# Softmax division moved behind P times V in both attentions of a two-layer hybrid decoder

## The chip, the cores and the metric

One Trainium2 chip, and one of its cores. The time is device time of one launch, in microseconds. The core has five engines that run beside each other, each in the order of its own queue: TensorE (PE; its weight loads are shown apart as PEld), VectorE (DVE), ScalarE (ACT), GpSimd (POOL) and SyncE (SP), which here issues nearly all DMAs. Engines wait for each other through semaphores. TensorE writes to PSUM, of which there are eight banks of 2 KB per partition; everything else lives in SBUF.

## What is computed

A trunk of two equal layers on one sequence of 1024 tokens, width 1024, all float32. Each layer normalises its input, projects it once to 1312 columns, and feeds three mixers from that: a sliding-window attention (window 128, six query heads, two key heads, a learned sink per head), a pooling mixer, and a causal latent attention (MLA, six heads). Their outputs are joined by one output projection, and a SwiGLU feed-forward block follows. The two softmaxes are what the change is about:

```python
# sliding window: per block of 128 queries, keys of this block and of the one before
s = jnp.where(mask, s + bias, -jnp.inf)
lse = jnp.logaddexp(jax.nn.logsumexp(s, axis=-1, keepdims=True), sk)   # sk: the sinks
p = jnp.exp(s - lse)
o = jnp.einsum('bnhgqk,bnkhd->bnqhgd', p.astype(v.dtype), vb)
# MLA: per block of 128 queries, all keys up to it
s = jnp.where(k_idx[None, :] <= qi[:, None], s, -jnp.inf)
p = jax.nn.softmax(s, axis=-1)
return jnp.einsum('bhqk,bkhd->bqhd', p.astype(v.dtype), v)
```

In both, a row of exponentials is divided by its sum (in the first, the sum holds the sink's term too) and then multiplied by V.

## The kernel before

Matrix products are split in two or three: an operand is rounded to a shorter float32 type (`hi`), the remainder is kept as `lo`, and hi·hi, hi·lo and lo·hi (or two of them) are summed in PSUM. The helper `split` (line 58) does this with one ScalarE cast and one VectorE subtraction, so all splits carry line 58.

Each layer has three phases. **`phase1`** (line 283) runs over eight tiles `t` of 128 tokens: normalise, transpose, project (lines 381 to 383), pooling mixer, and at its end the sliding-window attention of this tile. **`phase2`** (line 545) makes queries, keys and values of the MLA in `gen(t)`, and runs its attention in four sweeps `s` of 256 queries (two blocks `j` of 128); between heads it works off the output projection (`early_out`, at line 816 and lines 795 to 797, and `late_out`, line 819). **`phase34`** is the feed-forward block; it takes about 640 of the 1105 us of a layer and the change does not touch it.

**Sliding-window attention of one tile** (lines 503 to 541), for each of two groups `g` of three heads: QK to PSUM (513, 514); VectorE adds the bias into `Pt` (516) and takes the row maximum (518); ScalarE takes the exponentials, three instructions, whose row sums land in `sm` (521); VectorE takes the reciprocals (523); ScalarE multiplies `Pt` by them, three instructions (526); TensorE transposes `Pt` in 128-key blocks into the PSUM tile `tp` (532; pool `ps_tp`, one buffer); `split` makes `pT` from it; PV goes to `po` (536, 537), which holds the output transposed: value channels on partitions, queries along the free axis. The upper 64 partitions of `po` hold the product with V's remainder; ScalarE copies them to `ob` (539) and VectorE adds both halves into `xm[:, t, 0:3]` (540).

**MLA attention** (`attn`, lines 705 to 773), one head at a time: QK per block `j` (729 to 733); maximum (735, or 738 for the last sweep); exponentials with row sums (742; where the keys take two PSUM banks there are two sums, added at 744); reciprocal (746); `Pt` times the reciprocal (748), on VectorE for `j == 0` and in the third sweep for every third head's `j == 1`, else on GpSimd; transposes (756; `ps_tp`, two buffers), `split`, PV (765, 766), and the same joining of two halves (768, 770) into 64 partitions of `xm[:, 2s:2s+2, 5 + h//2]`. Two heads share a column of `xm`, one in each half of the partitions.

**What sets the order.** The program is written as one stream, and a planner in the framework (line 1295, `schedule_with_timeline_sim=True`) orders each engine's queue: it plays the program through with its own costs, and of the instructions that are ready takes the one earliest in the program, apart from those that the code pins (`issue_after`) or gives another place in that order (`high_priority`, as for `early_out`). So other instructions, or other durations in the planner's eyes, can give another order. SBUF is handed out as a stack of pools; `phase1` and `phase2` start at the same address, and a tile of a later phase waits for the tiles that lay at its place. Two dummy pools (`gap`, lines 298 and 302) move what stands above them.

**How the attention ends.** The first feed-forward weights are loaded to the place where `phase2` holds its small tiles (pool `late`: maxima, sums, `ob`), so this load (line 1102) waits for the last head. `late_out` reads `xm` of the last two tiles after it.

Of the kernel before, what the change touches and what calls it, by code (L numbers as in the profile page):

```python
# [11 lines left out]
F32 = mybir.dt.float32  # L12
# [3 lines left out]
AF = mybir.ActivationFunctionType  # L16
ALU = mybir.AluOpType
# [4 lines left out]
P = 128  # L22
# [260 lines left out]
def phase1(nc, tc, A, l, pool, split, f, bcast, G, setup):  # L283
    ve, sc, gp, te, sy = nc.vector, nc.scalar, nc.gpsimd, nc.tensor, nc.sync
    cosT, sinT = G["cosT"], G["sinT"]
    ident, xm, xrow, krr = G["ident"], G["xm"], G["xrow"], G["krr"]
    with ExitStack() as ph:
        gap = G["gap"]
        two = pool(ph, f"p1b_{l}", bufs=2)
        one = pool(ph, f"p1_{l}")  # L290
# [20 lines left out]
        ps_tp = pool(ph, f"p1tp_{l}", bufs=1, space=PSUM)  # L311
# [30 lines left out]
        with tc.high_priority() if l == 0 else nullcontext():  # L342
            if l == 0:
                head(0)
            for i, (c0, n) in enumerate(((0, 512), (512, 400), (912, 400))):
                for k in range(KT):
# [3 lines left out]
                    g = gn[:, k : k + 1]  # L350
# [10 lines left out]
        for g in range(4):  # L361
            o = 64 * (g % 2)
# [8 lines left out]
        for t in range(NT):  # L371
# [133 lines left out]
            for g in range(2):  # L505
                gs = slice(3 * g, 3 * g + 3)
                Pt = two.tile([P, 3, 264], F32, name="Pt")
                gp.tensor_copy(Pt[:, :, nk : nk + 1], G["sinks"][:, l, gs].unsqueeze(2))
                for i0, ni in ((0, 2), (2, 1)):
                    s = ps_sc.tile([P, 2, 256], F32, name="s")  # L510
                    for i in range(i0, i0 + ni):
                        h = 3 * g + i
                        te.matmul(s[:, i - i0, 0:nk], qs[:, h], kr5[:, 0, g, k0 : k0 + nk], start=True, stop=False)
                        te.matmul(s[:, i - i0, 0:nk], qs[:, h], kr5[:, 1, g, k0 : k0 + nk], start=False, stop=True)
                    h0 = 3 * g + i0
                    ve.tensor_tensor(out=Pt[:, i0 : i0 + ni, 0:nk], in0=s[:, 0:ni, 0:nk],
                                     in1=G["bias"][:, h0 : h0 + ni, 256 - nk : 256], op=ALU.add)
                ve.tensor_reduce(mx[:, gs], Pt[:, :, 0 : nk + 1], AX.X, ALU.max, negate=True)
                for i in range(3):
                    h = 3 * g + i  # L520
                    sc.activation(Pt[:, i, 0 : nk + 1], Pt[:, i, 0 : nk + 1], AF.Exp, bias=mx[:, h : h + 1],
                                  accum_out=sm[:, h : h + 1])
                ve.reciprocal(sm[:, gs], sm[:, gs])
                for i in range(3):
                    h = 3 * g + i
                    sc.activation(Pt[:, i, 0:nk], Pt[:, i, 0:nk], AF.Copy, scale=sm[:, h : h + 1])
                po = ps_o.tile([P, 512], F32, name="po")
                nb = nk // P
                for b in range(nb):
                    tp = ps_tp.tile([P, 4, P], F32, name="tp")  # L530
                    for i in range(3):
                        te.transpose(tp[:, i], Pt[:, i, b * P : (b + 1) * P], ident)
                    pT = two.tile([P, 2, 3, P], F32R, name="pT")
                    split(pT[:, 0], pT[:, 1], tp[:, 0:3])
                    vv = (vt if b == nb - 1 else vprev)[:, g].rearrange("p a d -> p (a d)")
                    te.matmul(po[:, 0:384], vv, pT[:, 0].rearrange("p a b -> p (a b)"), start=b == 0, stop=False)
                    te.matmul(po[:, 0:384], vv, pT[:, 1].rearrange("p a b -> p (a b)"), start=False, stop=b == nb - 1)
                ob = one.tile([P, 384], F32, name="ob")
                sc.copy(ob[0:64], po[64:128, 0:384])
                ve.tensor_tensor(out=xm[64 * g : 64 * g + 64, t, 0:3], in0=po[0:64, 0:384].rearrange("p (a b) -> p a b", a=3),  # L540
                                 in1=ob[0:64].rearrange("p (a b) -> p a b", a=3), op=ALU.add)
            vprev = vt


def phase2(nc, tc, A, l, pool, split, f, bcast, G):
# [3 lines left out]
    with ExitStack() as ph:  # L549
# [155 lines left out]
        def attn(s, heads):  # L705
            qTs = [q2[2 * s], q2[2 * s + 1]]
            for h in heads:
                Ps = []
                for j in range(2):
                    t = 2 * s + j  # L710
                    valid = (t + 1) * P
# [26 lines left out]
                        ve.tensor_reduce(mx[:, 0:1], outs[0][0], AX.X, ALU.max, negate=True)  # L738
                    if len(outs) == 2:
                        ve.tensor_tensor(out=mx[:, 0:1], in0=mx[:, 0:1], in1=mx[:, 1:2], op=ALU.min)  # L740
                    for i, (o, c0, n) in enumerate(outs):
                        sc.activation(Pt[:, c0 : c0 + n], o, AF.Exp, bias=mx[:, 0:1], accum_out=sm[:, i : i + 1])
                    if len(outs) == 2:
                        ve.tensor_tensor(out=sm[:, 0:1], in0=sm[:, 0:1], in1=sm[:, 1:2], op=ALU.add)
                    sm = sm[:, 0:1]
                    ve.reciprocal(sm, sm)
                    eng = ve if j == 0 or s == 2 and h % 3 == 0 else gp
                    eng.tensor_scalar(out=Pt[:, 0:valid], in0=Pt[:, 0:valid], scalar1=sm, scalar2=None, op0=ALU.mult)
                    Ps.append(Pt)
                po = ps_o.tile([P, 512], F32, name="po")  # L750
                for c in range(s + 1):
# [19 lines left out]
                    out=xm[r0 : r0 + 64, 2 * s : 2 * s + 2, 5 + h // 2],  # L771
                    in0=po[0:64, 0:256].rearrange("p (a b) -> p a b", a=2),
                    in1=ob[0:64].rearrange("p (a b) -> p a b", a=2), op=ALU.add)

        def both(s):
            streams = [gen(2 * s), gen(2 * s + 1)] if s < 4 else []
# [522 lines left out]
```

## Time and profile before

| | |
|---|---|
| time, median of 3 runs | 2216.93 us (2209.97 to 2217.36) |
| the profiled execution | 2210.4 us, span 2208.6 us, mean granted TensorE clock 0.985 |
| PE busy | 2114.1 us (96%), 10468 instructions |
| DVE busy | 1692.3 us (77%), 2595 |
| ACT busy | 1087.7 us (49%), 2300 |
| POOL busy | 976.2 us (44%), 916 |

All stages below are given in us from the span's start. The sliding-window attention runs in 45 to 241 and again in 1130 to 1350, the MLA sweeps in 241 to 445 and 1345 to 1545. A matmul's busy time includes its way through the array, and the next one starts long before it ends, so a PE that is 96% busy may still have room; the chain of waits, which follows the last instruction back to what released it, says better where PE sets the time. Windows give each engine's busy time in a stretch, with the number of instructions in brackets.

### The profile page before, as it was taken

To read this page: it belongs to the slowest core of one execution; us is meant where nothing else is said; L and a number is where in the kernel's file an instruction comes from. 1 tells how busy PE (TensorE), PEld (TensorE's weight loads), DVE (VectorE), ACT (ScalarE), POOL (GpSimd) and SP (SyncE) were. 2 spreads that over 40 slices of the span, in tenths; PEclk is the share of its full clock that TensorE was granted. 3 is DMA by queue.
4 is the path that set the end of the run, shared out by engine and by line. 5 is a ranking of instruction groups with operands and counts; after the bars stand their busy time and mean duration, and the time that the engine had idled before them with its cause. 6 is when DMAs were issued, how large, how long until landed. Compare 5 with 4: busy or idle time off the path is not lost.

```text
span 2208.6 us, 29772 instructions
## 1 busy us (share of the span) xinstructions
PE 2114.1 (96%) x10468; PEld 1766.5 (80%) x10468; DVE 1692.3 (77%) x2595; ACT 1087.7 (49%) x2300; POOL 976.2 (44%) x916
## 2 busy tenths in 40 slices
PE   7998999999999999999989988999999999999999
PEld 5887788877788888788868867988778888887887
DVE  5567888898988787765845678887998888877657
ACT  5778767563434333311257786665634343343111
POOL 1433647245544452532614344462465444425215
PEclk8999999999999999999999999999999999999999
DMA  7002221323534435975530022113234443359754
GB/s 220 1 1 80 82 77 39 106 96 133 181 134 166 149 125 198 412 296 188 200 113 1 1 95 77 68 49 102 96 144 165 144 171 134 142 217 412 278 200 162
DMA packets 137932, 312.16 MB, mean 141 GB/s; under 512 B 17297, under 2 KB 68152, under 8 KB 137784
## 3 DMA queue, kind: packets, MB, share of 16 engines
q1 hardware_dynamic: 137784, 310.27, 39.4%
q8 instruction: 83, 1.36, 0.3%
q14 instruction: 65, 0.53, 0.1%
HBM read 203.53 MB, written 106.70 MB: 140 GB/s over the span
## 4 chain that ended last, share of the span: by engine, by line
PE 70%; DVE 10%; DMA 8%; ACT 6%; POOL 3%; issue 2%; SPq 1%; ACTq 0%; POOLq 0%; DVEq 0%
PE gu L1149 10%; PE gu L1147 10%; PE gu L1148 10%; PE dn L994 5%; PE dn L996 5%; PE dn L995 5%; PE acc L381 3%; PE acc L382 3%; PE acc L383 3%; DMA rw<-in_w_down_dram 2%; PE tp L756 2%; DMA raw<-in_w_in_dram 1%; PE ss L732 1%; PE po L766 1%; DMA raw<-in_w_gate_dram 1%
## 5 line engine op out<-in xcount | busy, mean ns | idle before, releaser
L1149 PE MATMUL gu<-T,sb 128*128 128x512 f32 x704 | 274.8, 391 | 9.8 <-DVE sb L58 9.7
L1147 PE MATMUL gu<-T,sb 128*128 128x512 f32 x704 | 274.9, 390 | 4.6 <-ACT sb L58 2.5
L1148 PE MATMUL gu<-T,sb 128*128 128x512 f32 x704 | 274.0, 389 | 0.0
L994 PE MATMUL dn<-op,ga 128*128 128x512 f32 x616 | 241.3, 393 | 7.4 <-DMA ga<-gd 7.4
L995 PE MATMUL dn<-op,ga 128*128 128x512 f32 x616 | 241.4, 392 | 0.0
L996 PE MATMUL dn<-op,ga 128*128 128x512 f32 x616 | 240.6, 392 | 0.0
L58 ACT CAST go<-xm 128x512 fp32r<-128x512 f32 x154 | 95.1, 620 | 274.4 <-POOL xm L1181 94.2
L943 POOL TENSOR_TENSOR rw<-rw 128x1536 f32<-128x1536 f32 (+1 forms) x32 | 112.4, 3522 | 257.0 <-DVE op L953 163.5
L1124 POOL TENSOR_TENSOR xm<-raw 128x512 f32<-128x512 f32 x44 | 68.6, 1561 | 319.9 <-DMA raw<-in_w_up_dram 122.8
L952 ACT CAST op<-rw 128x1536 fp32r<-128x1536 f32 (+1 forms) x56 | 76.9, 1376 | 266.7 <-PE dn L996 253.8
L58 DVE TENSOR_TENSOR go<-xm,go 128x512 fp32r<-128x512 f32 x154 | 154.4, 1012 | 34.1 <-ACT go L58 30.1
L58 ACT CAST sb<-raw 128x512 fp32r<-128x512 f32 x180 | 110.4, 617 | 122.5 <-PE gu L1149 99.6
L1149 PEld LDWEIGHTS gu<-T,sb 128*128 128x128 f32 x704 | 132.1, 188 | 41.3 <-DVE sb L58 13.9
L1147 PEld LDWEIGHTS gu<-T,sb 128*128 128x128 f32 x704 | 132.2, 188 | 34.5 <-ACT sb L58 4.6
L1181 POOL TENSOR_TENSOR xm<-xm 128x512 f32<-128x512 f32 x88 | 143.3, 1637 | 30.4 <-DVE go L58 19.6
L1148 PEld LDWEIGHTS gu<-T,sb 128*128 128x128 f32 x704 | 132.2, 188 | 27.4
L58 DVE TENSOR_TENSOR sb<-raw,sb 128x512 fp32r<-128x512 f32 x180 | 152.9, 850 | 1.0
L953 DVE TENSOR_TENSOR op<-rw,op 128x1536 fp32r<-128x1536 f32 (+1 forms) x56 | 113.8, 2032 | 40.0 <-ACT op L952 40.0
L994 PEld LDWEIGHTS dn<-op,ga 128*128 128x128 f32 x616 | 116.7, 189 | 33.3 <-issue 7.3
L1147 PE MATMUL gu<-B,A 128*128 128x512 f32 x336 | 132.1, 393 | 4.4 <-ACT B L58 4.4
L995 PEld LDWEIGHTS dn<-op,ga 128*128 128x128 f32 x616 | 116.7, 189 | 24.4
L996 PEld LDWEIGHTS dn<-op,ga 128*128 128x128 f32 x616 | 116.7, 189 | 24.3
(322 smaller groups left out, 6102.5 us busy)
## 6 DMA issues: line engine op xcount, KB each, us to landing
gd<-go SPq DMA_DIRECT2D x154, 512.0 KB, 3.1
ga<-gd SPq DMA_DIRECT2D x154, 512.0 KB, 5.7
raw<-in_w_gate_dram SPq DMA_DIRECT2D x22, 1024.0 KB, 5.6
raw<-in_w_up_dram SPq DMA_DIRECT2D x22, 1024.0 KB, 6.5
rw<-in_w_down_dram SPq DMA_DIRECT2D x44, 512.0 KB, 8.1
xp<-xt SPq DMA_DIRECT2D x32, 256.0 KB, 2.0
old<-xp SPq DMA_DIRECT2D x16, 512.0 KB, 4.1
xp<-xm SPq DMA_DIRECT2D x16, 512.0 KB, 2.9
```

What stands on the lines that cost most here:

```text
L58: return sc.copy(hi, src), ve.tensor_tensor(out=lo, in0=src, in1=f(hi), op=ALU.subtract)
L943: gp.tensor_tensor(out=o, in0=a, in1=b, op=ALU.subtract)
L952: sc.copy(t[:, 0], q[b])
L953: ve.tensor_tensor(out=t[:, 1], in0=q[b], in1=f(t[:, 0]), op=ALU.subtract)
L994: te.matmul(acc, S_[:, j, 0, ts], T_[:, 0, j], start=j == 0, stop=False)
L995: te.matmul(acc, S_[:, j, 0, ts], T_[:, 1, j], start=False, stop=False)
L996: te.matmul(acc, S_[:, j, 1, ts], T_[:, 0, j], start=False, stop=j == h - 1)
L1124: gp.tensor_tensor(out=s1, in0=q["A21"], in1=q["A22"], op=ALU.add)
L1147: te.matmul(acc, s[:, 0, k], b[:, 0, k], start=k == 0, stop=False)
L1148: te.matmul(acc, s[:, 0, k], b[:, 1, k], start=False, stop=False)
L1149: te.matmul(acc, s[:, 1, k], b[:, 0, k], start=False, stop=k == HK - 1)
L1181: gp.tensor_tensor(out=q[o], in0=q[a], in1=q[b], op=op)
```

## The change

Neither attention scales `Pt` any more: the products with V run on the bare exponentials, and the finished output is multiplied by the reciprocal of the row sums. Since the output lies transposed (queries along the free axis), the reciprocals have to lie so too: they are spread over 64 columns per head by a GpSimd copy (`rec`), transposed by TensorE into a PSUM tile of the pool that the `Pt` transposes use, and VectorE multiplies `xm` in place by that tile. In phase 1 this is done once per tile, for all six heads: one reciprocal, one copy of 128x384, three transposes, one multiplication of 128x384. In phase 2 it is done once per pair of heads and sweep: one reciprocal of four sums, one copy of 128x256, two transposes, one multiplication of 128x256. The new tiles are `rec` (1536 bytes per partition, pool `one` of phase 1; 1024 bytes, pool `late` of phase 2) and `sums` (two buffers, pool `late`).

```diff
 # phase1, for each group g
-                ve.reciprocal(sm[:, gs], sm[:, gs])
-                for i in range(3):
-                    h = 3 * g + i
-                    sc.activation(Pt[:, i, 0:nk], Pt[:, i, 0:nk], AF.Copy, scale=sm[:, h : h + 1])
 ...
 # phase1, after both groups
+            ve.reciprocal(sm, sm)
+            rec = one.tile([P, 3, 2, 64], F32, name="rec")
+            gp.tensor_copy(rec, sm.rearrange("p (g i) -> p i g", g=2).unsqueeze(3).to_broadcast([P, 3, 2, 64]))
+            tp = ps_tp.tile([P, 4, P], F32, name="tp")
+            for i in range(3):
+                te.transpose(tp[:, i], rec[:, i].rearrange("p g d -> p (g d)"), ident)
+            ve.tensor_tensor(out=xm[:, t, 0:3], in0=xm[:, t, 0:3], in1=tp[:, 0:3], op=ALU.mult)
 ...
 # phase2, attn
+                if h % 2 == 0:
+                    G["sums"] = late.tile([P, 2, 2], F32, name="sums", bufs=2)
+                sums = G["sums"]
 ...
+                    total = sums[:, j, h % 2 : h % 2 + 1]
                     for i, (o, c0, n) in enumerate(outs):
-                        sc.activation(Pt[:, c0 : c0 + n], o, AF.Exp, bias=mx[:, 0:1], accum_out=sm[:, i : i + 1])
+                        sc.activation(Pt[:, c0 : c0 + n], o, AF.Exp, bias=mx[:, 0:1],
+                                      accum_out=sm[:, i : i + 1] if len(outs) == 2 else total)
                     if len(outs) == 2:
-                        ve.tensor_tensor(out=sm[:, 0:1], in0=sm[:, 0:1], in1=sm[:, 1:2], op=ALU.add)
-                    sm = sm[:, 0:1]
-                    ve.reciprocal(sm, sm)
-                    eng = ve if j == 0 or s == 2 and h % 3 == 0 else gp
-                    eng.tensor_scalar(out=Pt[:, 0:valid], in0=Pt[:, 0:valid], scalar1=sm, scalar2=None, op0=ALU.mult)
+                        ve.tensor_tensor(out=total, in0=sm[:, 0:1], in1=sm[:, 1:2], op=ALU.add)
 ...
+                if h % 2:
+                    ve.reciprocal(sums, sums)
+                    rec = late.tile([P, 2, 2, 64], F32, name="rec")
+                    gp.tensor_copy(rec, sums.unsqueeze(3).to_broadcast([P, 2, 2, 64]))
+                    tp = ps_tp.tile([P, 512], F32, name="tp")
+                    for j in range(2):
+                        te.transpose(tp[:, j * P : (j + 1) * P], rec[:, j].rearrange("p a d -> p (a d)"), ident)
+                    o = xm[:, 2 * s : 2 * s + 2, 5 + h // 2]
+                    ve.tensor_tensor(out=o, in0=o, in1=tp[:, 0 : 2 * P].rearrange("p (a b) -> p a b", a=2), op=ALU.mult)
```

## The prediction

> **What bounds the kernel now.** I read the page first, then the windows by stage, then the chain of waits stage by stage. The page:
>
> ```profile
> span 2208.6 us, 29772 instructions
> PE 2114.1 (96%) x10468; PEld 1766.5 (80%) x10468; DVE 1692.3 (77%) x2595; ACT 1087.7 (49%) x2300; POOL 976.2 (44%) x916
> PE 70%; DVE 10%; DMA 8%; ACT 6%; POOL 3%; issue 2%; SPq 1%; ACTq 0%; POOLq 0%; DVEq 0%
> ```
>
> TensorE sets 70% of the time, so whatever the change adds there counts where PE leads. Where it leads is seen in the windows of the attention stages (PE, PEld, DVE, ACT, POOL busy with counts; granted clock; DMA) and in the chain of three of them (70 to 185, 185 to 240, 325 to 375):
>
> ```profile
> 45.00:185.00 140.00, 135.77 (x783) 118.35 (x782) 86.50 (x201) 100.79 (x284) 53.15 (x120) 0.99 0.05 18
> 185.00:241.00 56.00, 48.00 (x259) 39.24 (x258) 46.89 (x94) 45.43 (x120) 29.24 (x54) 0.97 0.33 108
> 241.00:325.00 84.00, 81.77 (x498) 72.50 (x499) 71.55 (x169) 57.93 (x142) 44.01 (x44) 1.00 0.20 70
> 325.00:375.00 50.00, 45.48 (x307) 40.03 (x306) 45.54 (x115) 39.75 (x106) 33.19 (x32) 1.00 0.16 59
> 375.00:442.00 67.00, 66.66 (x432) 59.53 (x430) 54.37 (x87) 38.45 (x75) 23.36 (x19) 1.00 0.28 95
> 1279.00:1350.00 71.00, 60.39 (x306) 49.04 (x305) 53.75 (x108) 49.81 (x132) 29.86 (x50) 0.93 0.29 96
> 1431.00:1474.00 43.00, 38.92 (x245) 34.82 (x244) 36.63 (x92) 33.34 (x88) 33.18 (x32) 0.89 0.11 38
> ```
> ```profile
> by line: PE acc L382 23.7%; PE acc L383 23.6%; PE acc L381 23.6%; PE tq L406 4.6%; PE tp L532 4.5%; PE s L513 3.6%; PE th L339 3.2%; PE s L514 3.1%; PE po L536 2.8%; PE po L537 2.7%; PE ta L448 1.4%; PE ta L460 0.8%; DVE Pt L516 0.6%; PE po
> by line: DMA raw<-in_w_out_dram 12.8%; ACT Pt L526 9.0%; ACT Pt L521 8.1%; issue 6.9%; POOL ms L115 4.7%; ACT wo L58 4.3%; DVE ms L657 4.1%; ACT mh L58 3.4%; ACT qbh L577 3.1%; ACT pT L58 3.1%; ACT ob L539 2.7%; ACT kvh L577 2.4%; DVE ropea
> by line: DVE mx L735 12.4%; ACT Pt L742 11.7%; DVE pT L58 6.9%; issue 6.7%; ACT pT L58 5.9%; DMA raw<-in_w_out_dram 5.3%; PE ss L729 4.7%; PE ss L732 4.6%; PE ss L733 4.4%; DVE ms L657 3.4%; DVE Pt L748 3.3%; DVE kT L58 2.8%; POOL wot L834
> ```
>
> Each layer has two kinds of stretch. In three of them PE leads: the sliding window's first six tiles (45 to 185), the first two MLA sweeps (241 to 325) and the last (375 to 442). In two it doesn't: the **tail** of phase 1 (185 to 241, and 1279 to 1350), where ScalarE, DMA, and in layer 1 also POOL, take turns, and the **middle** of the MLA (325 to 375, and 1431 to 1474), where DVE is busy 91% and 85% of the time. The change takes work from ACT, DVE and POOL and gives some to PE: it can only earn in the loose stretches and must pay in the tight ones.
>
> **What is removed.** The first row is phase 1's scaling, the next two phase 2's, the last its reciprocal:
>
> ```profile
> L526 ACT ACTIVATE Pt<-Pt,sm x96: 389/497/528, 56.7 to 1325.3; 128x256 f32<-128x256 f32 x84, 128x128 f32<-128x128 f32 x12
> L748 DVE TENSOR_SCALAR Pt<-Pt,sm x52: 270/552/1155, 251.8 to 1518.8; 128x128 f32<-128x128 f32 x12, 128x384 f32<-128x384 f32 x12, 128x640 f32<-128x640 f32 x12, 128x896 f32<-128x896 f32 x12
> L748 POOL TENSOR_SCALAR Pt<-Pt,sm x44: 924/1604/3138, 253.1 to 1526.1; 128x256 f32<-128x256 f32 x12, 128x512 f32<-128x512 f32 x12, 128x1024 f32<-128x1024 f32 x12, 128x768 f32<-128x768 f32 x8
> L746 DVE RECIPROCAL sm<-sm x96: 134/156/167, 251.6 to 1525.9; 128x1 f32<-128x1 f32 x96
> ```
>
> That is 96 x 0.497 = 48 us off ACT, about 30 us off DVE beside 15 us of reciprocals, and some 75 us off POOL.
>
> **What is added.** Per tile of phase 1 (16 of them) one reciprocal, one POOL copy of 128x384, three transposes and one product of 128x384; per head pair and sweep (24) one reciprocal, one copy of 128x256, two transposes and one product of 128x256. The nearest rows are the four-transpose group of line 339 in the chain, a single transpose of line 756 by its own duration, POOL's broadcast copy, and the additions into `xm`, which also read PSUM with 384 and 256 elements per partition (they use 64 partitions; DVE's time goes by the free size in the rows that I compare, so I take them as they are):
>
> ```profile
> 84.39 0.44 PE th L339 x4
> L756 PE MATMUL tp<-ident,Pt x432: 270/273/449, 253.4 to 1540.6; 128*128 128x128 f32 x144
> L663 POOL COPY kn<-krr x16: 343/348/713, 209.9 to 1413.0; 128x192 f32<-128x192 f32 x16
> L540 DVE TENSOR_TENSOR xm<-po,ob x32: 540/550/553, 68.3 to 1346.9; 64x384 f32<-64x384 f32 x32
> L770 DVE TENSOR_TENSOR xm<-po,ob x48: 397/417/419, 265.4 to 1543.1; 64x256 f32<-64x256 f32 x48
> ```
>
> PE gets 16 x 3 + 24 x 2 = 96 transposes. Where PE is dense each takes 0.44 / 4 = 0.11 us of its queue, so 10.6 us in all; by their own duration of 0.273 us they would be 26 us, which is the upper bound. I take 0.11, because a transpose among other matmuls costs its distance to the next and not its way through the array.
>
> The Trainium skill (TensorE: Matmul & The Clock Gate, section Part 4: PE-mode transpose) puts such a transpose at about 275 ns in a kernel; the 273 ns of the row agrees as a duration, but not as a price: by the page the sum would be 96 x 0.275 = 26 us, by the distance in the chain 10.6 us, and the measurement decides.
>
> The tight stretches hold the following share, by where the removed instructions lie (windows of line 526 alone, then of line 746 alone, the first in 45 to 185 and the rest as they say):
>
> ```profile
> 45.00:185.00 140.00, 14.85 (x36) 0.99 0.05 18
> 241.00:325.00 84.00, 3.59 (x24) 1.00 0.20 70
> 325.00:375.00 50.00, 1.89 (x12) 1.00 0.16 59
> 1431.00:1474.00 43.00, 1.58 (x10) 0.89 0.11 38
> ```
>
> Thirty-six scalings are six tiles, so 18 transposes, 2.0 us. Twenty-four reciprocals are 12 heads, six pairs, 12 transposes, 1.3 us. The last sweep has three pairs, 0.7 us. Together 4.0 us per layer, **8 us lost** in the two layers. The other 24 transposes fall into the loose stretches, covered by PE's idle time there (56 - 48.0 us busy in the tail); without that cover they are 2.6 us more.
>
> **What is earned**, by the removed pieces that lie on the chain or on the leading engine. The windows of line 748 alone (DVE, POOL) for the two middles, and three single pieces of the chain:
>
> ```profile
> 325.00:375.00 50.00, 5.19 (x8) 9.31 (x4) 1.00 0.16 59
> 1431.00:1474.00 43.00, 4.35 (x7) 8.86 (x4) 0.89 0.11 38
> 266.37 1.64 POOL Pt L748
> 1295.78 1.21 ACT Pt L526 x3
> 443.15 8.43 DMA raw<-in_w_up_dram
> ```
>
> - Middle, layer 0: DVE loses 5.2 + 1.9 us and gets three pairs' reciprocal and product, 3 x (0.16 + 0.42) = 1.7: 5.4 us net. DVE falls to 40 us, level with ACT (39.75), so not all comes through: 4, between 0 and 5.4. POOL, which also makes the norms of the next sweep's queries there, loses 9.3 us.
> - Middle, layer 1: 4.35 + 1.6 - 1.5 = 4.4 us; I take 3, between 0 and 4.4.
> - Tail, layer 0: line 526 is 9.0% of 55 us, 5.0 us of the chain. DVE's 46.9 busy us are next in line and rise by 2 x 0.55. I take 3, between 0 and 5.0.
> - Tail, layer 1: 1.2 us on the chain; but POOL leads part of this stretch, and two copies of 128x384 go into its queue. A copy of 192 takes 0.35 us, so one of 384 lies between 0.35 and 0.7: about 1.0 us for two. Net 0, between -1.4 and 1.2.
> - The 1.64 us piece at 266: PE takes over at once, 1.5, between 0 and 1.6.
>
> Sum 11.5 us, between -1.4 and 17.6.
>
> **The end of the attention.** The first two feed-forward loads wait for the last head's small tiles, and the second of them (8.43 us, above) is on the chain; `rec` and `sums` will lie there too. The last row of sums is ready at 425, where its reciprocal starts, and the last addition into `xm` comes at 442:
>
> ```profile
> 425.13 0.16 DVE L746 RECIPROCAL sm<-sm 128x1 f32<-128x1 f32 x1 [0.70 <-ACT Pt L742]
> 442.24 0.43 DVE xm L770
> ```
>
> So copy and transposes have 17 us. Only the last product (0.42 us) comes after, and delays `late_out`, which runs beside that load. I take 0; without the cover it is 0.8 us for two layers.
>
> **SBUF.** `rec` lifts phase 1's later pools by 1536 bytes and phase 2's by about 1.1 KB. By pool sizes the one doubtful new neighbour is the odd tiles' `hT`, which comes to lie on weights of the last down-projection. Their last reader and the first cast into any `hT` are 25 us apart, so it costs 0, and up to that distance it stays so:
>
> ```profile
> L953 DVE TENSOR_TENSOR op<-rw,op x6: 1757/2120/2841, 1041.1 to 1084.4; 128x1536 fp32r<-128x1536 f32 x6
> L58 ACT CAST hT<-th x6: 573/586/597, 1109.6 to 1155.3; 128x512 fp32r<-128x512 f32 x6
> ```
>
> **The sum:** 8 lost, 11.5 earned: -3.5 us, between +9.4 (8 + 1.4) and -9.6 (8 - 17.6) with transposes at 0.11 us, and up to +27 if each cost its 0.273 us (26 + 1.4). The profiled execution took 2210.4 us, 1.8 beyond its span, and is 6.5 below the median shown; -3.5 gives 2207 by it and 2213.4 by the median. I forecast 2213.
>
> **The rivals.** *A, the relief goes further.* In the loose stretches PE not only waits, it also runs at half speed afterwards. The granted clock in three windows:
>
> ```profile
> 1290.00:1300.00 10.00, 9.03 (x38) 6.94 (x38) 7.30 (x16) 8.65 (x26) 0.47 (x2) 0.80 0.34 106
> 1330.00:1340.00 10.00, 9.45 (x42) 7.82 (x43) 6.00 (x13) 2.99 (x6) 0.00 (x0) 0.83 0.22 79
> 1465.00:1475.00 10.00, 8.59 (x35) 7.14 (x34) 4.79 (x12) 5.87 (x15) 5.96 (x4) 0.66 0.15 52
> ```
>
> They cost (0.20 + 0.17 + 0.34) x 10 = 7.1 us of PE. If a `Pt` that is ready up to 3 us sooner keeps PE fed there, this goes too, and the middles and tails give all: 8 - 17.6 - 7.1 = -17, 2200. For it: POOL's four scalings of 2.3 us stand in each middle between the norms that the next sweep waits for. Against it: ACT is close behind DVE. The Trainium skill (TensorE: Matmul & The Clock Gate, section What's actually happening) has the clock halved after an idle window of about 3.4 us; the 0.66 to 0.83 of these windows agree, and by it what counts is whether the waits get shorter than that.
>
> *B, PE waits for POOL.* Each group of transposes stands in PE's in-order queue behind a POOL copy that itself queues, and everything behind it on PE, the projections and QK, waits too; in phase 1 the single `tp` buffer is then held until the product is through. POOL's longest piece that can stand in front is the power of 12 columns:
>
> ```profile
> L115 POOL TENSOR_TENSOR ms<-ms,nhalf 128x12 f32<-128x12 f32 x16 | 38.2, 2394 | 0.8
> ```
>
> It runs in the tails and middles alone, where a layer has two tiles and three pairs, ten groups in all. A wait of 2.4 us at each is 24 us: 24 - 3.5 = +20, 2237. It decides the sign from 0.35 us per group (3.5 / 10), and a clear loss from 1.5 us. Against it: POOL is busy at most 77% anywhere (33.18 of 43), and loses more there than it gets. For it: the order is planned with the planner's costs, and a POOL that is later than planned stops PE.
>
> *C, nothing comes through.* The loose stretches end when other things come (DMA 12.8% of layer 0's tail, POOL's power 4.7%), DVE's relief is taken up by ACT, and the transposes are paid: +8, 2225, still no measurable change. The row of DMA speaks for it in the tails, DVE's 45.5 busy us of 50 speak against it in the middles.
>
> *D, another order.* The planner sees other instructions and reorders all of both attentions. This has no row; I give it 10 us to either side of C and of the forecast.
>
> **How the numbers follow.** What counts as no change is within 0.5%, 11 us, about what a measurement of this kernel can tell. The forecast of a small net gain (from -10 us, the lower end of the sum, to +3) has a chance of 0.34, A 0.27, B 0.17, C (+3 to +11) 0.14, D 0.08. Faster by over 0.5% is all of A, the edge of the forecast (0.05) and half of D: 0.36. Slower by over 0.5% is B, half of D and the edge of C (0.02): 0.23. The rest, 0.41, is no change. The range takes A's 2200 with some of its lower side and reaches towards B without holding it: 2193 to 2231; the forecast's own is 2207 to 2220.
>
> **What would show it.** Right: lines 526 and 748 gone; 96 new transposes 0.11 us apart in dense groups; the middle's DVE share down by 4 to 5 us in each layer and the stretch 3 to 4 us shorter; 45 to 185 and 375 to 442 each longer by 2 and 0.7 us. A: the same, with a granted clock of 1.00 in layer 1's middle. B: new waits of PE for POOL's `rec` or for a `tp` that the product still holds, over 1 us each. C: the middles as long as before, ACT or PE in DVE's place. Wrong altogether: a feed-forward block whose own length changes by over 3 us, since no step touches it.

## The result and the profile after

The changed kernel takes 2232.72 us (median, 2230.39 to 2234.32); the kernel before, timed beside it on the same chip, 2214.59 (2209.97 to 2217.36). The ratio is 1.0092, 95% interval 1.0065 to 1.0118: slower by 14 to 26 us. The prediction said 2213 and at most 2231, and put only 0.23 on slower by over 0.5%. The profiled execution took 2231.7 us. From its page, the span, the engines and the shares of the chain:

```profile
span 2229.9 us, 29824 instructions
PE 2126.2 (95%) x10564; PEld 1774.5 (80%) x10564; DVE 1681.7 (75%) x2495; ACT 1048.4 (47%) x2204; POOL 904.9 (41%) x912
PE 72%; DVE 10%; DMA 8%; ACT 5%; POOL 3%; issue 2%; SPq 0%; ACTq 0%; DVEq 0%; POOLq 0%
```

Every engine but PE has less to do than before (ACT by 39 us, POOL by 71, DVE by 11), PE has 96 matmuls more, and the span is 21.3 us longer.

To compare like with like I cut each layer at two events that both kernels have: the last copy into `ob` of the sliding window, and that of the MLA's last head. "Phase 1" runs up to the first (in layer 1 from the end of the feed-forward block), "MLA" from the first to the second.

| us, layer 0 / layer 1 | phase 1 | MLA |
|---|---|---|
| before | 250.2 / 242.0 | 192.0 / 196.1 |
| after | 258.6 / 242.6 | 200.9 / 197.9 |

That is 8.4 + 0.6 + 8.9 + 1.8 = 19.7 of the 21.3 us; the rest of each layer, the feed-forward block above all, is within 3 us of before. The loss lies in the attentions, and most of it in layer 0.

The cut doesn't divide equal work, though. Counted by line in the traces, the kernel before has started 180 matmuls of `phase2` ahead of it in layer 0 and 187 in layer 1, the kernel after 204 in both. How closely such matmuls follow each other is seen in 225 to 254 of the trace of after:

```profile
225.80 0.28 PE L650 MATMUL acc<-qbl,ch 128*128 128x192 f32 x1
225.91 0.27 PE L651 MATMUL acc<-qbh,cl 128*128 128x192 f32 x1
...
250.39 0.39 PE L808 MATMUL po<-wo,mh 128*128 128x512 f32 x1
250.62 0.40 PE L809 MATMUL po<-wo,mh 128*128 128x512 f32 x1
...
253.13 0.34 PE L650 MATMUL acc<-qbl,ch 128*128 128x384 f32 x1
253.31 0.34 PE L651 MATMUL acc<-qbh,cl 128*128 128x384 f32 x1
```

In layer 0 the difference is 12 with 192 columns, 0.11 us apart, and 12 with 384, 0.18 apart. So, as an estimate, 3 to 4 us of its longer "phase 1" are work of the MLA that was done sooner. A window with nearly the same work in both kernels runs from the last projection matmul of `phase1` to the MLA's last copy into `ob`; it has 30 matmuls more after, where 33 of the new transposes lie in it. First the two layers before, then after:

```profile
188.87:442.21 253.34, 238.25 (x1460) 207.48 (x1459) 215.69 (x457) 178.44 (x434) 127.15 (x140) 0.99 0.24 83
1278.79:1543.03 264.24, 246.16 (x1461) 213.10 (x1459) 214.73 (x457) 177.48 (x434) 125.45 (x140) 0.96 0.24 79
```
```profile
188.53:459.44 270.91, 249.51 (x1490) 214.69 (x1489) 204.88 (x408) 172.58 (x422) 89.56 (x131) 0.97 0.24 77
1296.95:1561.69 264.74, 246.28 (x1491) 213.20 (x1489) 203.27 (x408) 171.79 (x422) 89.42 (x131) 0.98 0.24 79
```

By it layer 0 loses 17.6 us and layer 1 half a microsecond. The windows of the kernel before, cut at its own events: layer 0's tail, its second, third and fourth sweep, and layer 1's third (PE, PEld, DVE, ACT, POOL busy; granted clock; DMA):

```profile
188.90:250.20 61.30, 52.98 (x280) 43.18 (x279) 50.37 (x100) 46.77 (x122) 26.55 (x46) 0.97 0.32 107
...
291.70:329.00 37.30, 36.96 (x234) 33.20 (x233) 32.61 (x72) 25.20 (x59) 20.90 (x20) 1.00 0.17 59
329.00:386.00 57.00, 52.82 (x356) 46.90 (x355) 51.26 (x124) 44.21 (x113) 39.67 (x34) 1.00 0.13 47
386.00:442.20 56.20, 55.86 (x359) 49.55 (x356) 45.06 (x71) 31.28 (x62) 16.88 (x17) 1.00 0.32 107
...
1425.80:1486.70 60.90, 56.82 (x355) 50.74 (x354) 51.31 (x124) 44.34 (x113) 38.77 (x34) 0.92 0.15 53
```

The same five of the kernel after:

```profile
188.50:258.60 70.10, 59.41 (x316) 47.69 (x315) 53.72 (x105) 46.19 (x119) 32.26 (x53) 0.98 0.31 98
...
294.90:342.40 47.50, 47.48 (x286) 41.48 (x285) 37.19 (x81) 27.61 (x71) 9.99 (x13) 1.00 0.25 88
342.40:401.90 59.50, 55.98 (x358) 50.38 (x357) 45.06 (x95) 41.88 (x103) 25.43 (x34) 0.94 0.15 50
401.90:459.40 57.50, 53.19 (x325) 45.74 (x323) 37.78 (x58) 28.54 (x57) 4.49 (x11) 0.97 0.26 87
...
1447.70:1504.30 56.60, 53.42 (x358) 47.51 (x357) 43.98 (x95) 41.51 (x104) 25.44 (x35) 1.00 0.16 53
```

Three things stand here. DVE has 6 to 7 us less to do in the third sweeps, somewhat more than forecast, but only layer 1's got shorter (by 4.3 us, with its clock back at 1.00); layer 0's got 2.5 us longer, and its clock fell from 1.00 to 0.94. The second sweep has 52 matmuls more (286 for 234) and takes 10.2 us longer, the fourth has 34 fewer (325 for 359) and is none the shorter: PE now stands 4.3 us in it, where it stood 0.3. And layer 0's tail, 61.3 us before, takes 70.1, with 36 matmuls more, among them nine of the new transposes and the 24 of the MLA.

### The profile page after: what moved, and what is told of

Its sections match the earlier page's. It is cut to its first block, busy times and chain, and to the rows that moved or that the text cites. A ratio compares the mean times of both kernels' runs of the same rounds, so it can differ in the third digit from the quotient of the medians.

```text
span 2229.9 us, 29824 instructions
## 1 busy us (share of the span) xinstructions
PE 2126.2 (95%) x10564; PEld 1774.5 (80%) x10564; DVE 1681.7 (75%) x2495; ACT 1048.4 (47%) x2204; POOL 904.9 (41%) x912
## 4 chain that ended last, share of the span: by engine, by line
PE 72%; DVE 10%; DMA 8%; ACT 5%; POOL 3%; issue 2%; SPq 0%; ACTq 0%; DVEq 0%; POOLq 0%
PE gu L1162 9%; PE gu L1161 9%; PE gu L1160 9%; PE dn L1007 5%; PE dn L1008 5%; PE dn L1009 5%; PE acc L381 3%; PE acc L382 3%; PE acc L383 3%; PE tp L760 2%; DVE sb L58 1%; PE po L770 1%; DMA raw<-in_w_in_dram 1%; PE po L810 1%; PE po L808 1%
## 5 line engine op out<-in xcount | busy, mean ns | idle before, releaser
L58 DVE TENSOR_TENSOR pT<-tp,pT 128x384 fp32r<-128x384 f32 (+1 forms) x180 | 108.4, 605 | 40.5 <-ACT pT L58 39.1
```

What stands on the lines that cost most here:

```text
L58: return sc.copy(hi, src), ve.tensor_tensor(out=lo, in0=src, in1=f(hi), op=ALU.subtract)
```

## The experiments

"Change" below is the whole change. The edits are shown shortened. The ratios are to the kernel before, timed beside each (medians 2211.3 to 2213.7 us). Kernels that leave the division out, or put its result elsewhere, return an undivided output; they are for the time alone.

**Halves.** The change in phase 1 alone, the change in the MLA alone:

```diff
 # e1_swa: phase1 of the change, attn of before      # e2_mla: attn of the change, phase1 of before
```

> Only the sliding-window attention divides late; the latent attention scales Pt as before. Theory O (the added work is small, and the loss comes from a new order in the MLA, whose last sweep lacks filler and lets PE stand 8 us more per layer): this kernel keeps the old MLA, so its last sweep stalls about 3 us as before and the time lies within 8 us of before (2207 to 2223); what is left is the tail of layer 0, +9 us if that loss belongs to phase 1's own edit. Theory R (PE and POOL wait for the rec tile wherever it is used): 16 of the 40 uses are here, so about 7 of the 18 us remain. Theory N (nothing but chance in the planner's order): any number within 15 us, with the gaps in places that the edit does not touch.

> Only the MLA divides late; the sliding window scales as before. Theory O: the last sweep of each layer (from the third sweep's last addition to the fourth's) stalls 11 us instead of 3, so +16 us for two layers, the middles earn 4 to 6 us in layer 1, and the sum is +8 to +18 us. Theory R: 24 of 40 uses, +11 us, and the waits stand at POOL's copy of rec. Theory N: e1 and this one do not add up to the 18 us of the whole change.

Measured: e1 2245.8 us, 1.0145 (1.0129 to 1.0161), more than the whole change; e2 2225.5, 1.0054 (1.0037 to 1.0071). The halves don't add up. In e1 the first MLA head ends 26 us later than before, in a place that the edit doesn't touch. GpSimd's waits in 180 to 300 of e1:

```profile
POOL C L622 <- PE po L533: 17.5, 1, 17.5
```

Tile `C` of phase 2 waits for the sliding window's last product with V. With `rec` below them, phase 1's later pools lie 1536 bytes higher, and by their order it is `vt`, which that product reads, that reaches into the place of `C`. So e1 measures a collision that the change does not have (there phase 2 lies 1088 bytes higher as well, and `C` is made at 217, in the kernel before at 218). Two more kernels are about that:

```diff
 # e6_lay: before, and unused tiles of the same sizes
+        gp.memset(one.tile([P, 384], F32, name="rec")[:, 0:1], 0.0)
+        gp.memset(late.tile([P, 272], F32, name="rec")[:, 0:1], 0.0)
 # e13_swa_gap: e1, but rec lies where a gap was
-        gap(ph, f"p1k_{l}", 2176)
+        recs = pool(ph, f"p1r_{l}")
+        gap(ph, f"p1k_{l}", 640)
```

> The kernel before, with an unused tile of 1536 bytes in phase 1's pool one and one of 1088 bytes in phase 2's pool late: the SBUF layout of the change without the change. My prediction has the move of SBUF at 0, so the time of before within 3 us. Theory S (the move makes tiles of phase 2 wait for tiles of phase 1 that lie at their place, as the sliding-window half of the change did for 17 us at tile C): 5 to 18 us slower, lost between the last projection and the second sweep, and POOL's or ACT's waits there name a matmul of phase 1.

> The sliding-window half alone once more, with its rec in place of 1536 of the 2176 unused bytes of the second gap, so that no tile moves. Theory S (the 32 us of the first try of this half came from the move of 1536 bytes, which put tile C over something that the last sliding-window tile reads): C is made at about 217 instead of 250, the first MLA head ends within 5 us of before, and the time is 2206 to 2222. If the sliding-window edit itself costs it: 2235 or more again.

Measured: e6 2213.0 us, 1.0002 (0.999 to 1.0015): the move alone costs nothing. e13 2255.3 us, 1.0191 (1.0176 to 1.0207): worse still, against the expectation. `C` is early now (208.6), but the gap was free space for good reason. The load of `rawqb`, which lies there in phase 2, in e13 and then in the kernel before:

```profile
L593 SPq DMA_DIRECT2D rawqb<-in_mla_w_qb_dram x2: 327/380/432, 243.2 to 244.2; - x2
```
```profile
L589 SPq DMA_DIRECT2D rawqb<-in_mla_w_qb_dram x2: 422/422/423, 188.0 to 188.4; - x2
```

And the transposes that read `rec` in e13, in 180 to 260:

```profile
L544 PE MATMUL tp<-ident,rec x12: 270/272/418, 182.2 to 243.7; 128*128 128x128 f32 x12
```

The MLA's query weights are asked for 55 us later: the second of the two loads goes where `rec` of the last sliding-window tile is read until 244.0, and is issued at 244.2. A third try gives phase 1's half the layout of the change:

```diff
 # e14_swa_lay: e1, and in phase2
+        gp.memset(late.tile([P, 272], F32, name="rec")[:, 0:1], 0.0)
```

> The sliding-window half alone, with 1088 unused bytes in phase 2's pool late, so that phase 1 and phase 2 lie to each other as in the whole change. Theory S (both tries of this half lost their time to tiles of phase 2 that waited for the place of a phase 1 tile): C and the loads of rawqb are as early as before, the first MLA head within 8 us of before, and the time is what the whole change has over the MLA half, +7 us: 2215 to 2224. If the sliding-window edit costs the time wherever rec lies: 2235 or more.

Measured: 2220.9 us, 1.0033 (1.0018 to 1.0049). Now the halves add up: 8 us here and 12 in e2, about the 20 of the change. Both attentions lose.

**Gain and price.** One kernel that only removes, one that only adds:

```diff
 # e3_bare: the change without these          # e5_pay: the change, and Pt scaled as before
-    ve.reciprocal / gp.tensor_copy(rec) / te.transpose(tp, rec) / ve.tensor_tensor(xm, xm, tp)
```

> Leaves the division out altogether: Pt is not scaled and nothing is added in its place, so the output is not divided by the row sums. It is the gain of the change alone. My prediction's sum has 11.5 us earned (between -1.4 and 17.6), so about 2203. Theory R: the loss is all in the added work, so this is faster by 10 to 18 us and its last sweep stalls 3 us. Theory O: the last sweep loses its filler here too, since the MLA's instructions come sooner, so it stalls 8 us or more per layer and the time is that of before within 8 us.

> Pays without earning: Pt is scaled by the reciprocals as before, and beside that the reciprocals, the rec copies, the 96 transposes and the products in xm are made as well (the product multiplies by the sum again, so the output is undivided). By my prediction's prices: 8 us on PE in the tight stretches and 2.6 in the loose ones, and DVE +24 x 0.42 + 16 x 0.55 us, so +8 to +15. Theory R: +18 + 11 = about +29 us, with PE's and POOL's waits at rec. Theory O: +8 to +15, and the last sweep keeps its filler because POOL's scalings still hold the heads back: stall 3 to 5 us.

Measured: e3 2197.9 us, 0.993 (0.9909 to 0.9951), so 11 to 20 us are earned; e5 2250.6, 1.0166 (1.0151 to 1.0181), so 33 to 40 us are paid. From e3 to the change it is 2232.7 - 2197.9 = 35 us. My sum had 11.5 earned and 8 paid. The gain was right in sum, the price four times too small.

**Which piece is paid for.** The added pieces one after the other:

```diff
 # e16_copies: the change without                # e17_noproduct: the change without
-    tp = ps_tp.tile(...); te.transpose(tp, rec)
-    ve.tensor_tensor(xm, xm, tp)                 -    ve.tensor_tensor(xm, xm, tp)
```

> Leaves out the transposes and the products: Pt is not scaled, the reciprocals are taken and spread into rec, and xm stays undivided. Of the 35 us between the kernel without any division (2198) and the change (2233). By my prediction's prices copies cost nothing: 2195 to 2202. If GpSimd's queue is what is spoilt: 2215 or more.

> Leaves out the products alone: reciprocals, copies and the 96 transposes are made, xm stays undivided. By my prediction's prices +8 to +11 us over the copies alone: 2205 to 2212, and the rest of the 35 us would be the products and what waits for them. If the transposes and the PSUM buffers that they hold are the cause: 2222 or more. If a transpose costs its full 0.27 us: 2198 + 26 = 2224.

| | median, us |
|---|---|
| nothing added (e3) | 2197.9 |
| reciprocals and copies (e16) | 2202.5 |
| and the transposes (e17) | 2202.6 |
| and the products (change) | 2232.7 |

The ratios of e16 and e17 are 0.995 (0.9931 to 0.9969) and 0.9958 (0.994 to 0.9976). The 96 transposes, the one price that I had worked out with care, cost 0.1 us by the medians and at most about 8 by the intervals, below the 2205 to 2212 that I expected of e17; the products cost 30 us (23 to 37 by the ratios). Their own time on DVE is 16 x 0.553 + 24 x 0.412 = 18.7 us:

```profile
L544 DVE TENSOR_TENSOR xm<-xm,tp x16: 541/553/556, 74.5 to 1364.8; 128x384 f32<-128x384 f32 x16
...
L786 DVE TENSOR_TENSOR xm<-xm,tp x24: 403/412/422, 277.5 to 1562.2; 128x256 f32<-128x256 f32 x24
```

**Is it GpSimd's copy?** In the change GpSimd stands at `rec` behind the transposes of the pair before, and the norms of queries and keys queue behind it. Who waits for the transposes of line 784:

```profile
  POOL rec L781: 23.8, 4
```

```diff
 # e7_act                                # e8_dve: reciprocal and copy in one
-    gp.tensor_copy(rec, ...)            -    ve.reciprocal(sums, sums); gp.tensor_copy(rec, sums...)
+    sc.copy(rec, ...)                   +    ve.reciprocal(rec, sums...)
```

> The whole change, with the copies into rec on ScalarE instead of GpSimd. Theory R (GpSimd's in-order queue stands at rec and the norms of the MLA's queries and keys queue behind it; rec stands for 24 us in four waits in the trace of the change): 8 to 18 us faster than the change, 2215 to 2225, with GpSimd's waits for rec gone and the early sweeps shorter. Theory O (order and added PE work, whoever spreads the sums): within 5 us of the change, 2228 to 2238. If ScalarE's queue now stands at rec instead: slower than the change.

> The whole change, with reciprocal and copy made by one VectorE reciprocal that reads the sums spread and writes rec: one instruction and one handover fewer per division. Theory R: as with ScalarE, 8 to 18 us faster than the change. Theory O: within 5 us of the change. The price of the wide reciprocals themselves on VectorE, 40 times about 0.3 to 0.5 us more, is 12 to 20 us of VectorE and shows in the third sweep if VectorE leads there.

Measured: e7 2236.3 us, 1.0106 (1.0083 to 1.0129), as the change; e8 2269.5, 1.0256 (1.0234 to 1.0277). GpSimd is not the cause: with ScalarE in its place nothing is won, though ScalarE waits at `rec` for the transposes only 1.4 us in all. (In e9, below, GpSimd waits there for 63 us, and the kernel is no slower than the change.) e8 paid for something else, the wide reciprocals:

```profile
L539 DVE RECIPROCAL rec<-sm x16: 2536/2552/2554, 61.8 to 1360.2; 128x384 f32<-128x384 f32 x16
...
L779 DVE RECIPROCAL rec<-sums x24: 1730/1744/1754, 276.8 to 1575.3; 128x256 f32<-128x256 f32 x24
```

That is 16 x 2.55 + 24 x 1.74 = 83 us of DVE, four to seven times the 12 to 20 that I expected.

**What about the products?** Two kernels separate three answers: DVE's time, `xm` complete later, or something that both leave.

```diff
 # e21_aside: the products beside xm
-    ve.tensor_tensor(out=xm[...], in0=xm[...], in1=tp, op=ALU.mult)
+    ve.tensor_tensor(out=rec, in0=xm[...], in1=tp, op=ALU.mult)
 # e18_pool: the products on GpSimd, tp given back by a ScalarE copy
+    sc.copy(rec, tp)
+    gp.tensor_tensor(out=xm[...], in0=xm[...], in1=rec, op=ALU.mult)
```

> The whole change, but the 40 products write into rec instead of xm, so xm stays undivided and the output projection's reads of it no longer wait for copy, transposes and product. Theory V (VectorE's time and queue: the products stand in front of splits and maxima that PE waits for): 2226 to 2235, as the change. Theory X (xm is complete later, and the planner and the chip put the output projection's filler elsewhere): 2202 to 2210, as without the products.

> The whole change with the products on GpSimd, after a ScalarE copy of tp into rec: VectorE loses 19 us, ScalarE gets 40 copies of about 0.45 us, GpSimd 40 products of about 0.6 to 0.9 us, and tp comes free at the copy. Theory V: 2203 to 2214, level with or faster than before. Theory X: 2230 to 2245, since the products' results come later still.

Measured: e21 2241.2 us, 1.0126 (1.0108 to 1.0144); e18 2231.1, 1.0091 (1.0066 to 1.0116). As whole kernels both stay at the change's time or above it; neither of the two theories fits both. e21 rules out that readers wait for a later `xm`: nothing that reads it waits there. For DVE's time e18 has to be read by its two attentions, below.

What the slow MLAs have in common, and e18's has not, is a PSUM buffer that stays shut for long. One division of the change, in 322 to 331: the transposes of `rec`, the pair's additions into `xm`, the product.

```profile
L784 PE MATMUL tp<-ident,rec x2: 273/273/273, 323.0 to 323.1; 128*128 128x128 f32 x2
L774 DVE TENSOR_TENSOR xm<-po,ob x2: 408/413/418, 324.1 to 329.1; 64x256 f32<-64x256 f32 x2
L786 DVE TENSOR_TENSOR xm<-xm,tp x1: 411/411/411, 330.2 to 330.2; 128x256 f32<-128x256 f32 x1
```

The transposes are done at 323.4, because the sums are known long before. The product has to wait for the second head's addition, which starts at 329.1, and reads `tp` until 330.6. For 7.6 us one of the two buffers that every `Pt` transpose goes through is shut. In e18, in 327 to 329, the buffer is given back after 1.2 us:

```profile
L785 PE MATMUL tp<-ident,rec x2: 272/272/273, 327.5 to 327.6; 128*128 128x128 f32 x2
...
L787 ACT COPY rec<-tp x1: 366/366/366, 328.3 to 328.3; 128x256 f32<-128x256 f32 x1
```

**A later place in the program.** With the division written one head later its product finds its addition done, so `tp` is held for less; with the other one, the same in phase 1 by one tile:

```diff
 # e9_late: in attn                       # and behind attn(s, (h,)):
-    if h % 2: <division>                 +    divide(1 if h % 2 else 0)
+    if h % 2: owed.append((s, h, sums))  +    if h == 5: divide(0)
 # e15_both_late: also in phase1: the division of tile t at the end of tile t + 1
 # e11_mla_late: e9 with phase1 of before
```

> The whole change, with the MLA's divisions written one head later in the program (the last pair of a sweep at its end as before), so that in the planner's order everything of the next head comes first. Theory R: the copy finds its sums ready, GpSimd no longer stands at rec, 5 to 12 us faster than the change. Theory O: the order changes again; the transposes cost the same 5 us per layer, so within 8 us of the change, with no pattern in where it goes.

> The whole change with both divisions later in the program: in the MLA one head, in the sliding window one tile. If the place of the division in the program is the cause in both: the MLA's part 5 us less than the change, as measured, and the tail of phase 1 shorter by 4 to 9 us per layer (70 us back towards 61 to 66), so 2212 to 2222. If the place matters in the MLA alone: as with the MLA's divisions later, 2224 to 2230.

> The MLA half alone, with its divisions one head later in the program; the sliding window scales Pt as before. If halves and places add up: the MLA half cost 12 us, the later place earned 5, so about +7 us, 2215 to 2222. If it is the planner's order and nothing that adds: anywhere between 2205 and 2235.

Measured: e9 2227.1 us, 1.0062 (1.0045 to 1.008); e15 2221.1, 1.0038 (1.0025 to 1.0052); e11 2215.0, 1.0011 (1.0002 to 1.0021). The place is worth 10 us in the MLA half alone (e2 to e11). The table has the sum of the holds (from the start of a division's first transpose to the end of what frees `tp`, taken in pairs by order) per layer, and the length of the MLA:

| | hold of `tp`, us, layer 0 / 1 | `phase2` matmuls ahead of the cut | MLA, us, layer 0 / 1 |
|---|---|---|---|
| e3, nothing added | 0 | 191 / 187 | 189.4 / 193.3 |
| e16, copies | 0 | 189 / 181 | 190.6 / 195.5 |
| e17, no products | 0 | 186 / 186 | 192.7 / 192.8 |
| e18, copied out | 12 / 14 | 197 / 204 | 193.1 / 193.3 |
| e9, later | 36 / 36 | 204 / 204 | 196.1 / 195.7 |
| e11, later, MLA alone | 41 / 36 | 187 / 178 | 196.4 / 197.0 |
| e15, later | 39 / 39 | 171 / 171 | 203.3 / 198.2 |
| e21, beside `xm` | 66 / 68 | 204 / 204 | 198.9 / 202.4 |
| change | 75 / 75 | 204 / 204 | 200.9 / 197.9 |
| e7, copies on ScalarE | 75 / 77 | 204 / 208 | 198.1 / 199.8 |
| e2, MLA alone | 75 / 82 | 187 / 178 | 200.9 / 200.4 |

The MLA gets longer as the buffer is held longer: 189 to 196 us without a hold, 198 to 202 with 66 us and more. e15 stands out, but of its MLA 33 matmuls fewer lie ahead of the cut than of e9's. At the distances above (15 of them have 512 columns, 0.23 us apart, six 384 and twelve 192) that is 6 us, an estimate: most of the 7.2 us by which e15's is longer in layer 0, and more than the 2.5 in layer 1.

A single row proves little: the MLA of before, which has no division, takes 192.0 / 196.1 us in the kernel before, 192.2 / 198.6 in e6 and 196.8 / 194.7 in e14. The firmest pair is e2 and e11, with phase 1 of before and the same counts: both make all products and transposes, and the one with half the hold is 10 us faster as a whole kernel. DVE's time can't be much of it. In e8 it grew by 24 x (1.74 - 0.18) = 37 us in the two MLAs, which take 14.8 us longer than those of the change; by that, an estimate, the 24 x 0.412 = 10 us of the products are worth 4 us, of the 13.3 us between e17 and the change. What isn't isolated is the hold from the order: a later place moves both, and e18, which shortens the hold in the same place, also takes the product to another engine. The hold is the reading that fits all of them.

Phase 1 doesn't follow this rule. With the division a tile later (e15) it takes 249.6 / 232.5 instead of 258.6 / 242.6, of which 6 us in each layer are again the 33 matmuls; with the product on GpSimd (e18) 262.9 / 248.4, though both free the single `tp` sooner (10 and 16 to 19 us of holds per layer for 25). e18 puts a ScalarE copy of 0.48 us and a GpSimd product of 1.01 us into each tile instead. Which of them costs it there, I didn't separate. As whole kernels the gain of e18's MLA and the loss of its phase 1 cancel.

**The filler.** Between heads PE works off `late_out`. Its last matmul of a sum into `tp` (tiles 0 to 5; a tile of that name in another pool, `ps_f`), in the fourth sweep of the kernel before, of the change, and of e10:

```profile
L797 PE MATMUL tp<-wot,cl x30: 389/393/398, 388.3 to 433.9; 128*128 128x512 f32 x30
```
```profile
L810 PE MATMUL tp<-wot,cl x24: 389/393/397, 401.8 to 433.8; 128*128 128x512 f32 x24
```
```profile
L813 PE MATMUL tp<-wot,cl x30: 389/393/398, 392.9 to 443.8; 128*128 128x512 f32 x30
```

The last head of the kernel before ends at 442.2, that of the change at 459.4: the change goes 25 us without filler, before it was 8. e10 holds ten of its twelve groups of nine matmuls back, two per head:

```diff
 # e10_hold: in late_out, for t < 6 and n         # e12_mla_late_hold: the same on e11
-    outmm(po, mh, ml, ...)
+    with tc.issue_after(done[HOLD[2 * t + n]].ins): outmm(po, mh, ml, ...)
```

> The whole change, with the twelve groups of nine matmuls that late_out has for tiles 0 to 5 held back: two behind each head from the third sweep's last to the fourth sweep's fourth. In the trace of before their last matmul comes 8 us before the last head's end, in that of the change 26 us before it, and the last sweep's idle is 11 us instead of 3. Theory O (PE stands in the last three heads because its filler was used up before): the last sweep 4 to 8 us shorter in each layer, so 2217 to 2225. If the last sweep is bound by its heads' own chain: its length stays at 57 us and the time within 3 us of the change.

> The MLA half alone, divisions one head later, late_out's matmuls held back as in the other kernel. If both causes are as I think: 8 to 12 us less than without the hold, 2205 to 2212, which would be level with before or just under. If the hold takes filler from sweeps that need it: as without the hold or slower.

Measured: e10 2228.1 us, 1.0067 (1.0052 to 1.0082), about 5 us less than the change, which the intervals don't quite separate, where I expected 8 to 16; its MLA takes 195.9 / 198.5. e12 2215.0, 1.0009 (0.9996 to 1.0021), as e11, where I expected 8 to 12 less. So I take the early filler for a consequence: with the buffer shut the planner fills the gaps of the second sweep (its 52 matmuls more), and the last one lacks what was used there. Where the buffer is held less (e11), holding the filler back wins nothing.

## Why the prediction was wrong

- **What is earned** was right in sum, 11.5 forecast, 11 to 20 measured (e3), but by luck, for its places were wrong. The sum had 8.5 us in layer 0 and 3 in layer 1. In e3's trace phase 1 and MLA together take 443.8 us in layer 0, 442.2 before, and 430.1 in layer 1, 438.2 before: nothing in the one, 8 us in the other. e16 and e17 show the same (447.7 / 425.6 and 442.7 / 431.1). In the change layer 1's third sweep gave 4.3 us and its clock went to 1.00, as rival A had it; layer 0's gave nothing, its clock fell to 0.94, and its tail lost 9.
- **The transposes** stand 0.11 us apart (323.0 and 323.1 above), so the row was the right one; yet the 8 us that I charged for them don't show (e16 to e17, 0.1 us). The stretch up to the last projection, for which I forecast 2 us more per layer, takes 0.3 us less in layer 0 (to 188.53, before to 188.87) and, from the end of the feed-forward block, 1.9 more in layer 1 (175.8 for 173.9). By the Trainium skill's 0.275 us, measured there on bf16 (TensorE: Matmul & The Clock Gate, Part 4: PE-mode transpose), it would, as an estimate, have been 26 us; the measurement is against that as a price too.
- **The step that failed** is the cost of what is added: the product entered the sum as 0.42 us of DVE in the middles, 0.55 in the tails and nothing elsewhere. It cost 30 us. Its own time was sized right (0.412 and 0.553 us). What was left out is what it makes others wait for, in the MLA by the best reading the PSUM buffer that it shuts: between e17 and the change the two MLAs grew by 13.3 us, and with the 18 matmuls per layer that the change does ahead of the cut (5 us in both, an estimate) by some 18. Phase 1 keeps some 8 us, whose cause is open. "So copy and transposes have 17 us" was written as a comfort for the end of the attention. In the first three sweeps such a lead is the defect: transposes that are early by 6 to 9 us hold `tp` for as long. In the last sweep the holds are 2 to 3 us.
- **Rival B** named the held `tp` in passing and ended at 2237, 4 us from the result, but for another reason: it let PE wait for GpSimd's copy. e7 takes the copy off GpSimd and nothing changes. Its count was off as well: the power of 12 columns does not run in the tails and middles alone, four of its eight in layer 0 start at 260, 264, 301 and 306, in the first two sweeps. PE's waits in the trace don't name the held buffer, since the planner had put other work into the gaps. It shows as work done sooner and missed later.
- **Rival C** (nothing comes through) is out: e3 shows that it comes through. **Rival D** (another order) is part of the mechanism: the filler's place moved, and holding it back recovers about 5 us at best (e10). The order alone keeps an uncertainty of some us: before, e6 and e14 have the same MLA in the program, and its time in a layer differs by up to 4.8 us.
- **SBUF** at 0 was right for the change (e6), and by luck: the same edit with `rec` alone in phase 1, or in the place of a gap, makes the first MLA head end 26 us (e1) and 34 us (e13) later.
- **Feed-forward** within 3 us, as said.
- **A slip:** some 75 us off POOL should read 44 x 1.604 = 71; no term of the sum used it.

Open: what the product costs phase 1 with (12.8 us in both layers between e17 and the change by the cut, some 8 without the MLA's matmuls), the layer 0 tail, and how much of the MLA's loss is the order. The pieces that won, phase 1's division a tile later and the MLA's `tp` copied out, were not run together; none of the kernels that divide was faster than the one before, and e11 and e12, which divide late in the MLA alone, were level with it.

## What to carry to other kernels

Price an added step not only by its instructions but by the buffer that it holds, from its first write to its last read; a producer that is much too early makes that long, and in a pool of two it leaves all others who use the pool a single buffer. Compare stages at cuts with the same work on both sides; an event that both kernels have is not enough. Remove and add in separate kernels, and add the pieces one by one: that found in three runs what no wait in the trace named. When half a change is run alone, look first whether its tiles lie where they lay in the whole.

## What was not expected of the hardware

A reciprocal over a wide tile takes 2.55 us for 128x384 and 1.74 us for 128x256 (e8), so (2.552 - 1.744) / 128 = 6.3 ns per element, where the product of 128x384 takes 0.553 us in all. The Trainium skill (VectorE: DVE Perf Modes, section "First, the fixed hardware budget") has the reciprocal as an iterative division with a repeat count of 8; the measured slope is about six times the product's (0.553 - 0.412) / 128 = 1.1 ns. Reciprocals belong on the narrow sums, and the spreading after them: GpSimd's broadcast copy of 128x384 took 0.504 us.
